# Channel mixers of a two-layer encoder trunk: two of the four weight-block sums formed on GpSimd in place of VectorE

## Chip, cores and metric

The kernel runs on one core of one Trainium2 chip. The metric is the device time of one execution in microseconds (us), the median of the runs shown. TensorE is called PE, its weight loads PEld, VectorE DVE, ScalarE ACT, GpSimd POOL and SyncE SP.

## What is computed

A trunk of two layers over 512 tokens of width 1024 in float32. Each layer has a token mixer (layer 0: a matrix memory and a memory attention; layer 1: a band attention and a memory attention) and then a channel mixer. The change lies in the channel mixers, which compute, with `D_FF` = 2816:

```
def conv_ffn(h, w_up, conv_w, conv_b, w_down):
    u, g = jnp.split(h @ w_up, 2, axis=-1)
    g = causal_dwconv(g, conv_w, conv_b)
    return (jax.nn.silu(g) * u) @ w_down
...
        x = x + conv_ffn(rmsnorm(x, norm_ffn_g[l]), ffn_w_up[l], ffn_conv_w[l], ffn_conv_b[l], ffn_w_down[l])
```

## The kernel before

**Numbers.** Every float32 operand of a matmul is split in two: a high part, rounded by ACT (a CAST, line 140), and a low part, source less high part, by DVE (line 141). Each product is then three matmuls (`mm3`, lines 194 to 196). High and low parts of weights live in tiles `wh`/`wl` or `fh`/`fl`, activations in `u`.

**The channel mixer.** The 2816 hidden columns are 22 tiles of 128 (`j` = 0 to 21). Tiles 0 to 4 are computed plainly (`plain`). Tiles 5 to 21 (`later`, one `step` each, 17 in each layer) take one level of a seven-product block scheme: the weights of the tile's up columns and gate columns are cut in halves of the inner dimension, a11 and a12 (up), a21 and a22 (gate), the activations were cut and combined once by `forms`, and seven half-size products replace eight. For that, four sums of weight blocks are formed for each tile, each 128 partitions by 512 elements, all in line 888:

- s1 = a21 + a22 (`sums`; the gate's halves)
- s2 = s1 - a11 (`sums`)
- s3 = a11 - a21 (`sum_third`; up less gate)
- s4 = a12 - s2 (`sum_fourth`)

The raw gate blocks lie in one big `pt` tile (two slots, in turn), the raw up blocks in `wr`, and the four sums in a second `pt` tile that all steps share: s1 and s3 in its first half (`s13`), s2 and s4 in its second (`s24`). So in rows of the profile `pt<-pt` is s1, `pt<-pt,wr` s2, and `pt<-wr,pt` s3 or s4.

**The order of a step.** The orders on PE, ACT and DVE are written out by hand (`tc.manual_schedule`, lines 817 to 822); POOL's and SP's orders are the scheduler's. In step j PE runs the products of tile j (call `w`), while DVE and ACT form the blocks of tile j+1 (`nxt`) and finish the outputs of tile j-1 (`tail`). PE's order: a11 into bank r1, a12 into r2, s2 into r1, s1 into r3 (`psc`), s3 into r1, down products of an earlier group (`ptr`, one of them in steps 5 to 8, two in steps 9 to 20, as the table `UNITS` gives them by tile), a22 into r1, s4 into r3. The bank r1 is used four times a step; before each new use ACT has copied it out (lines 842 and 834).

The chain that the prediction follows lies in the first half of a step and belongs to the tail: DVE adds r3 to a result (line 938) and splits s4 (line 141), then does the two taps of the convolution (line 685, two instructions); ACT then applies the SiLU (line 950) and, behind it in its queue, copies the s2 product out of r1 (line 834), upon which PE may write the s3 product into r1. Later in the step DVE forms s1 and s2 (line 888), gates (line 953), forms s3 (line 888), and splits; near its end ACT and DVE split the whole tile s13 (`split_sums`: `wh<-pt`, `wl<-pt`), then DVE forms s4, and both split the gate's half and, ahead of step 7 and of each step from 9 on, a tile of down weights (`split_down`, `wl<-wr`).

**POOL's queue.** In the mixers POOL held only DMA issues: the accumulating stores of down products (line 778, behind an ACT copy, line 777), and in steps 5 to 16 of layer 0 a pair of copies for the bias rows of layer 1 (lines 1271 and 1273, `more_rows`); the second of a pair waits until the first has landed.

Of the kernel before, what the change touches and what calls it, by code (L numbers as in the profile page):

```python
# [13 lines left out]
ALU = mybir.AluOpType  # L14
# [40 lines left out]
def trunk(  # L55
# [19 lines left out]
    V, A, G = nc.vector, nc.scalar, nc.gpsimd  # L75
# [18 lines left out]
    def ps(tag):  # L94
        count[0] += 1
        return psum.tile([P, S], F32, tag=tag, name=f"p{tag}{count[0]}", bufs=pbufs[tag])
# [6 lines left out]
    def small(n=4, dtype=F32):  # L103
# [15 lines left out]
        out=maskf, in_=maskf, pattern=[[1, P]], base=0, channel_multiplier=-1,  # L119
# [746 lines left out]
    class Forms:  # L866
# [17 lines left out]
            split(hi, lo, src)  # L884
            return hi, lo

        def sub(self, o, x, y, op=ALU.subtract):
            V.tensor_tensor(out=o, in0=x, in1=y, op=op)  # L888

        def sums(self):  # L890
            a21, a22 = self.halves(self.gate)
            s1, s2 = self.halves(self.s13)[0], self.halves(self.s24)[0]
            self.sub(s1, a21, a22, ALU.add)
            self.sub(s2, s1, self.halves(self.up)[0])

        def split_second(self):
            self.s2 = self.form(self.halves(self.s24)[0])

        def sum_third(self):
            self.sub(self.halves(self.s13)[1], self.halves(self.up)[0], self.halves(self.gate)[0])  # L900

        def split_up(self):
            self.a11, self.a12 = zip(*(self.halves(t) for t in parts(self.up, block=0)))
# [379 lines left out]
    for j in range(KT):  # L1283
        wh, wl = weights(rows(ffn_w_down[0], j * P, P, FT - LAST, FT), LAST, P)
        o = ps("mm")
# [255 lines left out]
```

## Time and profile before

| what | value |
|---|---|
| time, three runs | median 1179.55 us (1179.12 to 1180.36) |
| the profiled execution's own time | 1178.89 us |
| its span (first to last instruction) | 1177.2 us |
| PE / DVE / ACT / POOL busy in the span | 99% / 80% / 62% / 11% |
| steps of layer 0, steps of layer 1 | about 340 to 575 us, about 895 to 1128 us |
| a step with two down products, a step with one | 15.0 us, 12.3 us |

The profile is of one execution, so sums go against 1178.89 us. A row of the timeline gives the start and the duration in us, engine, line and operation, the tile written and the tiles read, and in brackets the idle time ahead of it with what ended it. Neighbouring instructions of DVE and ACT overlap by almost 0.1 us in these rows, so that 0.69 us of one is 0.61 us from start to start. Ends of matmuls are modelled: starts say more.

### The profile page before, as it was taken

The numbers are of one execution on the slowest core, as the hardware profiler recorded it, in microseconds if no ns is written. First come the engines' busy times: TensorE is split into PE (matmuls) and PEld (weight loads), VectorE is DVE, ScalarE is ACT, GpSimd is POOL, SyncE is SP. The second block draws the span as 40 slices with busy tenths as digits, with TensorE's granted clock in tenths as the row PEclk, the third lists the DMA queues.
The fourth block names the chain that finished last, engine by engine and source line by source line (L and its number), as shares of the span: only waits on it lengthen the run. The fifth ranks groups of instructions, "written<-read, shape, count | busy, mean of one in ns | idle before, by whom it ended". The sixth has DMA issues, their size and how long they took to land.

```text
span 1177.2 us, 18659 instructions
## 1 busy us (share of the span) xinstructions
PE 1167.7 (99%) x7007; PEld 1033.4 (88%) x7007; DVE 941.1 (80%) x1685; ACT 730.3 (62%) x1295; POOL 129.6 (11%) x222
## 2 busy tenths in 40 slices
PE   9999999999999999999999999999999999999997
PEld 9988888888889999999888888888889999999986
DVE  6877688887979887777698888897897887777755
ACT  6548677654656656665666667776565665666545
POOL 1111101000021111111020000101001011110100
PEclk9999999999999999999999999999999999999999
DMA  8645325243267766665564312335426456566551
GB/s 301 206 108 136 94 55 152 76 140 120 90 157 153 190 165 162 163 144 128 149 200 126 90 54 85 105 100 179 142 90 153 108 140 140 143 144 144 126 161 72
DMA packets 200445, 158.64 MB, mean 135 GB/s; under 512 B 8377, under 2 KB 180383, under 8 KB 200355
## 3 DMA queue, kind: packets, MB, share of 16 engines
q1 hardware_dynamic: 184194, 119.87, 34.5%
q0 software_dynamic: 15584, 36.67, 15.8%
q8 instruction: 55, 0.90, 0.3%
q10 hardware_dynamic: 576, 0.92, 0.2%
q14 instruction: 36, 0.29, 0.1%
HBM read 128.89 MB, written 32.46 MB: 137 GB/s over the span
## 4 chain that ended last, share of the span: by engine, by line
PE 95%; DVE 3%; ACT 1%; issue 0%; POOL 0%; POOLq 0%; DVEq 0%; ACTq 0%
PE pmm L194 18%; PE pmm L195 18%; PE pmm L196 18%; PE ptr L195 6%; PE ptr L194 6%; PE ptr L196 6%; PE psc L196 5%; PE psc L195 5%; PE psc L194 5%; PE psc L544 2%; PE ptr L1365 1%; PE ptr L1386 1%; PE ptr L1387 1%; PE ptr L627 1%; PE ptr L613 0%; DVE pt L141 0%
## 5 line engine op out<-in xcount | busy, mean ns | idle before, releaser
L194 PE MATMUL pmm<-u,wh 128*128 128x512 f32 (+1 forms) x968 | 333.0, 344 | 0.2 <-ACT u L140 0.2
L196 PE MATMUL pmm<-u,wl 128*128 128x512 f32 (+1 forms) x968 | 330.8, 342 | 0.0
L195 PE MATMUL pmm<-u,wh 128*128 128x512 f32 (+1 forms) x968 | 330.5, 342 | 0.0
L141 DVE TENSOR_TENSOR wl<-wr,wh 128x1024 fp32r<-128x1024 f32 (+3 forms) x172 | 199.8, 1163 | 82.0 <-ACT wh L140 81.5
L140 ACT CAST wh<-wr 128x1024 fp32r<-128x1024 f32 (+3 forms) x172 | 171.9, 1001 | 93.1 <-PE pmm L195 39.6
L196 PEld LDWEIGHTS pmm<-u,wl 128*128 128x128 f32 x968 | 181.9, 188 | 20.8
L194 PEld LDWEIGHTS pmm<-u,wh 128*128 128x128 f32 x968 | 181.8, 188 | 18.7 <-ACT u L140 1.1
L195 PEld LDWEIGHTS pmm<-u,wh 128*128 128x128 f32 x968 | 182.0, 188 | 18.4 <-DVE u L141 0.5
L194 PE MATMUL ptr<-u,wh 128*128 128x512 f32 x272 | 106.4, 391 | 0.0
L195 PE MATMUL ptr<-u,wh 128*128 128x512 f32 x272 | 106.2, 390 | 0.0
L196 PE MATMUL ptr<-u,wl 128*128 128x512 f32 x272 | 105.8, 389 | 0.0
L778 POOL DMA_DIRECT2D xspill<-t x64 | 55.5, 867 | 432.1 <-ACT t L777 419.6
L834 ACT COPY t<-pmm 128x256 f32<-128x256 f32 x102 | 38.2, 374 | 76.7 <-PE pmm L196 76.5
L141 DVE TENSOR_TENSOR u<-t,u 128x512 fp32r<-128x512 f32 (+1 forms) x94 | 54.2, 600 | 35.4 <-ACT u L140 35.4
L194 PE MATMUL pmm<-u,fh 128*128 128x256 f32 x272 | 75.4, 277 | 0.0
L195 PE MATMUL pmm<-u,fh 128*128 128x256 f32 x272 | 75.2, 277 | 0.0
L196 PE MATMUL pmm<-u,fl 128*128 128x256 f32 x272 | 75.1, 276 | 0.0
L196 PE MATMUL psc<-u,wl 128*128 128x256 f32 (+1 forms) x232 | 75.1, 324 | 0.0
L195 PE MATMUL psc<-u,wh 128*128 128x256 f32 (+1 forms) x232 | 75.1, 324 | 0.0
L194 PE MATMUL psc<-u,wh 128*128 128x256 f32 (+1 forms) x232 | 74.9, 324 | 0.0
L141 DVE TENSOR_TENSOR fl<-pt,fh 128x512 fp32r<-128x512 f32 x102 | 70.4, 690 | 5.1 <-ACT fh L140 1.4
L140 ACT CAST fh<-pt 128x512 fp32r<-128x512 f32 x102 | 62.8, 616 | 9.2 <-DVE pt L888 6.0
(334 smaller groups left out, 2509.1 us busy)
## 6 DMA issues: line engine op xcount, KB each, us to landing
wr<-in_ffn_w_up_dram SPq DMA_DIRECT2D x54, 512.0 KB, 6.0
wr<-in_ffn_w_down_dram SPq DMA_DIRECT2D x38, 512.0 KB, 5.5
pt<-in_ffn_w_up_dram SPq DMA_DIRECT2D x34, 512.0 KB, 7.7
xspill<-t POOLq DMA_DIRECT2D x64, 256.0 KB, 4.3
wr<-in_a_w_in_dram SPq DMA_DIRECT2D x20, 512.0 KB, 3.8
wr<-in_w_kv_dram SPq DMA_DIRECT2D x12, 512.0 KB, 4.1
xspill<-fh POOLq DMA_DIRECT2D x16, 256.0 KB, 2.6
xspill<-fl POOLq DMA_DIRECT2D x16, 256.0 KB, 3.1
```

Source lines behind the costliest of these rows:

```text
L140: high = A.copy(hi, src) if on_act else V.tensor_copy(hi, src)
L141: low = V.tensor_tensor(out=lo, in0=src, in1=f(hi), op=ALU.subtract)
L194: nc.tensor.matmul(o, lh, rh, start=first, stop=False, skip_group_check=more)
L195: nc.tensor.matmul(o, lh, rl, start=False, stop=False, skip_group_check=more)
L196: nc.tensor.matmul(o, ll, rh, start=False, stop=last, skip_group_check=more)
L544: nc.tensor.matmul(o, a, b, start=first and i == 0, stop=i == 1)
L627: nc.tensor.matmul(o2, vs[a][:, 2 * hp + h, :], p[h][:, a, :], start=i == 0, stop=i == 3)
L778: G.dma_start(xspill[j], t, accum_op=ALU.add)
L834: A.copy(o, r[:, :H])
L1365: nc.tensor.transpose(tp[:, b * P : (b + 1) * P], es[T, h][:, b * P : (b + 1) * P], ident)
L1386: nc.tensor.matmul(o2[:, s * P :], w, hi_at(pts[h], s, s, TT - s), start=s == 0, stop=False)
L1387: nc.tensor.matmul(o2[:, s * P :], w, lo_at(pts[h], s, s, TT - s), start=False, stop=s == TT - 1)
```

## The change

`sub`, the helper of line 888, takes an engine. s1 and s3 go to POOL; s2 and s4 stay on DVE. Operands, tiles and values are the same.

```
-        def sub(self, o, x, y, op=ALU.subtract):
-            V.tensor_tensor(out=o, in0=x, in1=y, op=op)
+        def sub(self, o, x, y, op=ALU.subtract, on=V):
+            on.tensor_tensor(out=o, in0=x, in1=y, op=op)
...
-            self.sub(s1, a21, a22, ALU.add)
+            self.sub(s1, a21, a22, ALU.add, G)
             self.sub(s2, s1, self.halves(self.up)[0])
...
-            self.sub(self.halves(self.s13)[1], self.halves(self.up)[0], self.halves(self.gate)[0])
+            self.sub(self.halves(self.s13)[1], self.halves(self.up)[0], self.halves(self.gate)[0], on=G)
```

34 sums s1 and 34 sums s3 leave DVE's queue and enter POOL's. PE's order is the same, ACT's the same but for one cast in layer 1 that moves ahead of a copy. Three places show the rest.

**Step 7 of layer 0, DVE** (from the second tap to the split of the up weights; `t_3869` is the tail's tile, `pt_3237` the sums, `pt_3236` the gate's blocks, `wr_3866` the up blocks):

```order
 L685 SCALAR_TENSOR_TENSOR t_3869<-t_3723,cols_799,t_3869 128x510
 L845 TENSOR_TENSOR t_3878<-t_3878,pmm_3876 128x256
-L888 TENSOR_TENSOR pt_3237<-pt_3236 128x512
 L888 TENSOR_TENSOR pt_3237<-pt_3237,wr_3866 128x512
 L953 TENSOR_TENSOR t_3869<-t_3721,t_3869 128x512
 L141 TENSOR_TENSOR fl_3939<-pt_3237,fh_3938 128x512
-L888 TENSOR_TENSOR pt_3237<-wr_3866,pt_3236 128x512
 L141 TENSOR_TENSOR u_3957<-t_3869,u_3956 128x512
 L141 TENSOR_TENSOR wl_3961<-wr_3866,wh_3960 128x1024
```

Two instructions have gone, both behind the taps of this step; nothing else moved.

**The same two sums on POOL** (tile 8's), behind the accumulating store of step 6's down product and the first copy of a bias row:

```order
 L778 DMA xspill<-t_3830 128x512
 L1271 DMA rep_3862<-in_b_rel_row_dram 128x640
+L888 TENSOR_TENSOR pt_3237<-pt_3236 128x512
+L888 TENSOR_TENSOR pt_3237<-wr_3866,pt_3236 128x512
 L1273 DMA rep_3862<-maskf 64x64
 L778 DMA xspill<-t_3987 128x512
```

Both sums stand directly behind the store that came at the end of step 6, so they may run while DVE is at the beginning of step 7. In layer 1 the order is the same without lines 1271 and 1273.

**A step with two down products, on POOL** (the sums of tile 13, formed around the start of step 12; `t_4660` and `t_4667` are the two stores of step 11):

```order
 L1273 DMA rep_4524<-maskf 64x64
 L778 DMA xspill<-t_4660 128x512
+L888 TENSOR_TENSOR pt_3237<-pt_3236 128x512
+L888 TENSOR_TENSOR pt_3237<-wr_4703,pt_3236 128x512
 L778 DMA xspill<-t_4667 128x512
```

Here the sums stand between the two stores.

**The first steps of layer 0, on POOL:**

```order
+L888 TENSOR_TENSOR pt_3237<-wr_3531,pt_3236 128x512
+L1271 DMA rep_3561<-in_b_rel_row_dram 128x640
+L1273 DMA rep_3561<-maskf 64x64
 L778 DMA xspill<-t_3475 128x512
 L778 DMA xspill<-t_3491 128x512
+L888 TENSOR_TENSOR pt_3237<-pt_3236 128x512
+L888 TENSOR_TENSOR pt_3237<-wr_3565,pt_3236 128x512
 L778 DMA xspill<-t_3511 128x512
 L778 DMA xspill<-t_3527 128x512
-L1271 DMA rep_3561<-in_b_rel_row_dram 128x640
-L1273 DMA rep_3561<-maskf 64x64
```

The first pair of bias copies has moved ahead of four stores.

## The prediction, as put on record

> **What bounds the kernel now.** I read the busy times first, then what PE waits for, then the starts of PE's matmuls.
>
> ```profile
> span 1177.2 us, 18659 instructions
> PE 1167.7 (99%) x7007; PEld 1033.4 (88%) x7007; DVE 941.1 (80%) x1685; ACT 730.3 (62%) x1295; POOL 129.6 (11%) x222
> 250.00:575.00 325.00, 324.84 (x2125) 294.91 (x2124) 268.60 (x399) 196.03 (x323) 46.37 (x64) 1.00 0.59 147
> 805.00:1125.00 320.00, 320.00 (x2090) 291.18 (x2090) 265.82 (x395) 194.38 (x320) 31.62 (x40) 1.00 0.56 136
> PE pmm L453 <- DVE mcf L127: 1.1, 1, 1.1
> PE pmm L196 <- DVE u L141: 0.4, 2, 0.2
> ```
>
> The columns of the two windows are length, then busy time (and instructions) of PE, PEld, DVE, ACT and POOL, then clock, DMA share and GB/s. They hold the mixers' steps, and PE is busy in them throughout, at a granted clock of 1.00. The last two rows are the longest waits of PE by what it waited for, 1.1 us at the start and 0.4 us. So PE is the bound; DVE, at 83% (268.6 of 325), has room on average.
>
> A busy PE can still hide small waits, as its ends are modelled. The starts tell:
>
> ```profile
> 370.44 0.28 PE L196 MATMUL psc<-u,wl 128*128 128x256 f32 x1
> 370.56 0.28 PE L194 MATMUL pmm<-u,wh 128*128 128x256 f32 x1
> ```
>
> A matmul shown as 0.28 us is followed after 0.12 by the next, here and in other steps I looked at. What PE could gain in the steps is therefore about nothing. The change can only cost, where it makes PE wait, or be hidden.
>
> **What is removed.** DVE loses 34 sums s1 and 34 of the sums in the second row:
>
> ```profile
> L888 DVE TENSOR_TENSOR pt<-pt x34: 682/684/693, 240.0 to 1111.5; 128x512 f32<-128x512 f32 x34
> L888 DVE TENSOR_TENSOR pt<-wr,pt x68: 683/686/698, 334.2 to 1119.7; 128x512 f32<-128x512 f32 x68
> ```
>
> 34 x 0.684 + 34 x 0.686 = 46.6 us of DVE. They stand behind the taps of their step, and before the next taps DVE waits for ACT anyway (rows below), so they buy PE nothing: 0 us.
>
> **What is added.** No row shows POOL adding two tensors. Nearest are a write of 512 elements and a select of 128:
>
> ```profile
> L524 POOL MEMSET u<- 64x512 f32 x24 | 12.7, 531 | 137.9 <-PE psc L544 69.9 <-PE pmm L195 40.3 <-ACT t L1354 23.0
> 190.00 0.30 POOL L1172 TENSOR_SCALAR_AFFINE_SELECT t<-t 128x128 f32<-128x128 f32 x1
> ```
>
> A sum passes 512 elements three times, two in and one out. As cheap as the memset, it takes 0.53 us; with three passes in a row, 1.6 us. I take two passes, 1.1 us (the memset is the nearest row, and a write can run beside the reads), and keep both ends. [...]
>
> At 1.1 us POOL has time. Its wait as such costs nothing if the sum is started early:
>
> ```profile
> 430.29 0.92 POOL L778 DMA_DIRECT2D xspill<-t  x1 [2.07 <-ACT t L777]
> 438.69 0.69 DVE L888 TENSOR_TENSOR pt<-pt,wr 128x512 f32<-128x512 f32 x1
> ```
>
> In step 12, s1 and s3 stand behind this store, from 431.2, and DVE needs s1 at about 438, for s2, 7 us later; s3 is needed later still. Behind the two sums wait only stores and bias copies. The first pair of copies moves ahead of two stores and makes them wait up to
>
> ```profile
> POOL rep L1273 <- DMA rep<-in_b_rel_row_dram: 84.7, 12, 8.2
> ```
>
> 8.2 us once; their buffers come back eight tiles later in the ring `t`, over a step away. I count 0; without that cover ACT's next tile would wait out the rest, at most 8 us once.
>
> **Where the two engines collide.** The same trace shows POOL and DVE getting in each other's way:
>
> ```profile
> 188.54 0.78 DVE L141 TENSOR_TENSOR u<-t,u 128x512 fp32r<-128x512 f32 x1
> 188.75 0.72 POOL L1172 TENSOR_SCALAR_AFFINE_SELECT t<-t 128x128 f32<-128x128 f32 x1
> 233.56 0.33 POOL L1172 TENSOR_SCALAR_AFFINE_SELECT t<-t 128x128 f32<-128x128 f32 x1 [1.45 <-ACT t L1170]
> 233.66 0.65 DVE L141 TENSOR_TENSOR pt<-t,pt 128x384 fp32r<-128x384 f32 x1
> L141 DVE TENSOR_TENSOR wl<-wr,wh 128x384 fp32r<-128x384 f32 x4 | 2.2, 548 | 0.0
> ```
>
> A select that takes 0.30 us alone takes 0.72 beside a DVE instruction with two inputs in SBUF, and ends 0.15 us after that one's end (189.32). The other way round, a DVE split of 384 elements behind a running select takes 0.65 in place of 0.55. I read this as taking turns: the later of the two waits for the earlier. Nearly all DVE work of a step has two such inputs. [...]
>
> So each step pays two turns of G (one sum's time) on DVE, around its beginning. PE feels it through one chain: DVE taps, ACT SiLU, ACT copy out of bank r1, PE's s3 product into r1. Its slack decides. In step 12:
>
> ```profile
> 431.13 0.69 DVE L888 TENSOR_TENSOR pt<-wr,pt 128x512 f32<-128x512 f32 x1
> 431.74 0.68 DVE L141 TENSOR_TENSOR fl<-pt,fh 128x512 fp32r<-128x512 f32 x1
> 433.68 1.23 DVE L141 TENSOR_TENSOR wl<-wr,wh 128x1024 fp32r<-128x1024 f32 x1 [1.26 <-ACT wh L140]
> 437.55 0.63 ACT L950 ACTIVATE t<-t 128x512 f32<-128x512 f32 x1 [0.97 <-DVE t L685]
> 438.92 0.37 ACT L834 COPY t<-pmm 128x256 f32<-128x256 f32 x1 [0.74 <-PE pmm L196]
> 440.08 0.28 PE L194 MATMUL pmm<-u,wh 128*128 128x256 f32 x1
> ```
>
> The SiLU ends at 438.18, the copy could start at 438.92 (0.74), and it ends at 439.29, 0.79 before PE's start: the slack is 1.53 us. The sums start when the first row ends (431.82); with a split (0.61) between them the wide split follows at 431.82 + 2G + 0.61, against 433.68 before: late by 2G - 1.25, since its wait for ACT takes up the rest. At G = 1.1 that is 0.95, under 1.53: PE waits 0. The 11 steps 10 to 20 of each layer are of this kind.
>
> Step 7 has no such gap and less slack:
>
> ```profile
> 364.54 0.89 POOL L1271 DMA_DIRECT2D rep<-in_b_rel_row_dram  x1
> 364.93 0.68 DVE L141 TENSOR_TENSOR fl<-pt,fh 128x512 fp32r<-128x512 f32 x1
> 365.53 1.22 DVE L141 TENSOR_TENSOR wl<-wr,wh 128x1024 fp32r<-128x1024 f32 x1
> 366.67 0.41 DVE L938 TENSOR_TENSOR t<-t,psc 128x256 f32<-128x256 f32 x1
> 367.00 0.69 DVE L141 TENSOR_TENSOR fl<-pt,fh 128x512 fp32r<-128x512 f32 x1
> 367.60 1.53 DVE L685 SCALAR_TENSOR_TENSOR t<-t,cols,t 128x511 f32<-128x511 f32 x2
> 369.23 0.63 ACT L950 ACTIVATE t<-t 128x512 f32<-128x512 f32 x1 [2.17 <-DVE t L685]
> 369.76 0.36 ACT L834 COPY t<-pmm 128x256 f32<-128x256 f32 x1
> ```
>
> The copy runs right behind the SiLU and ends at 370.12, 0.44 before PE's 370.56 (quoted above); the two ACT rows overlap by 0.1, so I take 0.35 as slack. s1 comes to POOL's head at 365.43 and gets its turn at 365.62; then the wide split (1.22), s3 beside line 938 (one input in PSUM), the second split (0.61), the taps: 365.62 + 2G + 1.83 against 367.60, late by 2G - 0.15; were the wide split first and s1 behind it, it would be the same. PE waits 2G - 0.5 = **1.7 us** at G = 1.1. Steps 7 and 9 of each layer are so: 4 x 1.7 = 6.8 us.
>
> Step 8 lies between:
>
> ```profile
> 377.20 0.69 DVE L141 TENSOR_TENSOR fl<-pt,fh 128x512 fp32r<-128x512 f32 x1
> 378.74 1.53 DVE L685 SCALAR_TENSOR_TENSOR t<-t,cols,t 128x511 f32<-128x511 f32 x2
> 380.37 0.63 ACT L950 ACTIVATE t<-t 128x512 f32<-128x512 f32 x1 [1.04 <-DVE t L685]
> 381.67 0.38 ACT L834 COPY t<-pmm 128x256 f32<-128x256 f32 x1 [0.67 <-PE pmm L196]
> 382.83 0.28 PE L194 MATMUL pmm<-u,wh 128*128 128x256 f32 x1
> ```
>
> Slack 0.67 + 0.78 = 1.45; the taps follow at 377.89 + 2G + 0.61, late by 2G - 0.24 = 1.96: PE waits 0.5, twice 1.0 us. Step 6 has a little more slack and an idle gap of DVE; I count it as 0.
>
> Sum: 6.8 + 1.0 = **7.8 us**. 1178.89 + 7.8 = 1186.7; the median of the three runs stands 0.66 above the profiled one, so 1187.3.
>
> **Rivals.**
>
> *No collision that matters (no change).* DVE's instructions follow each other closely, and if POOL gets in only beside those with an input in PSUM, or the two share the port finely, the delay halves: 2G becomes G, step 7 pays 0.6, the others nothing, 4 x 0.6 = 2.4 us at most, 1179.6 to 1182. It is decided in step 7: a lateness under 0.35 us there costs nothing. Against it is the select that held DVE up.
>
> *The sums are longer than I think.* With 2G - 1.25 against 1.53, the 22 wide steps begin to pay from G = 1.39. At 1.6 they pay 0.42 each, 9.2 us; steps 7 and 9 pay 2.7, 10.8 us; step 8 1.5, 3.0: 23 us, 1202.5. At G = 0.53 steps 7 and 9 pay 0.56, 2.2 us: 1181.8.
>
> *Faster.* It would need PE waits that the 46.6 us of DVE time remove. In the windows PE has none; outside the steps only the first s1 of each layer leaves DVE, 0.7 us each. Were both on the path, 1178.1. A gain of 0.2% isn't in reach by this; only waits that the starts don't show would give it.
>
> **How the numbers follow.** A measurement of this kernel can tell about 0.2%, 2.4 us, from no change. The forecast (steps 6 to 9 pay, the wide ones not or hardly; 1182 to 1195): 0.48. No collision that matters: 0.26. Long sums, over 1195: 0.22. Faster: 0.04. The range goes from 1178.5, where nothing collides, to 1205, just beyond G = 1.6; I leave out the faster case and half of the long sums, 0.15. Slower by over 0.2%: 0.48 + 0.22 = 0.70; same 0.26; faster 0.04.
>
> **What would show it.** POOL rows of line 888 near 1.1 us alone, longer beside DVE; DVE splits and taps at the start of steps lengthened by about 1 us; SiLUs of steps 7 and 9 about 2 us later against PE's s1 product, with a gap of 1.7 us between PE's starts ahead of s3, and no gap in steps 10 to 20. I am wrong if DVE rows keep their 0.69 us, if POOL's take over 1.4 us, or if PE waits elsewhere: for s2, whose DVE instruction now waits for POOL, or for a buffer.

## The result, and the profile after

The changed kernel takes 1193.9 us (median of 4 runs, 1192.43 to 1195.92), the kernel before 1179.95 (4 runs, 1179.12 to 1181.59): 1.0121 times as long, 95% interval 1.0109 to 1.0134. That is slower by 14 us, inside the range and on the side that was forecast, and about twice the forecast 7.8 us.

The page of the changed kernel, and the longest waits of PE (total us, times, longest):

```profile
span 1192.6 us, 18788 instructions
PE 1172.1 (98%) x7007; PEld 1035.7 (87%) x7007; DVE 958.0 (80%) x1617; ACT 727.3 (61%) x1295; POOL 238.0 (20%) x290
...
PE pmm L194 <- ACT t L834: 10.3, 7, 2.4
PE pmm L453 <- DVE mcf L127: 1.1, 1, 1.1
PE ptr L194 <- ACT t L777: 0.5, 1, 0.5
```

PE now waits seven times for line 834, ACT's copy out of r1: that is the chain that the prediction named. DVE never waits for a sum of POOL's: its waits for POOL, 1.3 us in all, are those for line 1172, and the kernel before has them too. DVE has 68 instructions fewer and is busy for 17 us longer (958.0 against 941.1): its rows hold time in which it was shut out. The sums, by the instructions of line 888 (shortest, median, longest ns):

```profile
L888 POOL TENSOR_TENSOR pt<-pt x34: 1285/1667/1994, 239.9 to 1120.4; 128x512 f32<-128x512 f32 x34
L888 POOL TENSOR_TENSOR pt<-wr,pt x34: 1282/1742/3829, 329.4 to 1122.0; 128x512 f32<-128x512 f32 x34
```

G, a sum's time with nobody in its way, is 1.28 us, the shortest row. A longer row isn't always a wait. The pair of step 5 of layer 1 has no DVE instruction beside it:

```profile
903.16 1.60 POOL L888 TENSOR_TENSOR pt<-pt 128x512 f32<-128x512 f32 x1
904.42 1.60 POOL L888 TENSOR_TENSOR pt<-wr,pt 128x512 f32<-128x512 f32 x1
```

Its rows show 1.60 us, but the starts lie 1.26 apart: on POOL, too, starts say more than lengths. Step 7 of layer 0, the timelines of POOL, DVE, ACT and PE:

```profile
366.82 1.62 POOL L888 TENSOR_TENSOR pt<-pt 128x512 f32<-128x512 f32 x1
368.07 1.62 POOL L888 TENSOR_TENSOR pt<-wr,pt 128x512 f32<-128x512 f32 x1
```

```profile
366.61 3.64 DVE L141 TENSOR_TENSOR fl<-pt,fh 128x512 fp32r<-128x512 f32 x1
370.17 1.21 DVE L141 TENSOR_TENSOR wl<-wr,wh 128x1024 fp32r<-128x1024 f32 x1
371.31 0.41 DVE L938 TENSOR_TENSOR t<-t,psc 128x256 f32<-128x256 f32 x1
371.64 0.68 DVE L141 TENSOR_TENSOR fl<-pt,fh 128x512 fp32r<-128x512 f32 x1
372.24 1.52 DVE L685 SCALAR_TENSOR_TENSOR t<-t,cols,t 128x511 f32<-128x511 f32 x2
```

```profile
373.86 0.63 ACT L950 ACTIVATE t<-t 128x512 f32<-128x512 f32 x1 [5.12 <-DVE t L685]
374.39 0.35 ACT L834 COPY t<-pmm 128x256 f32<-128x256 f32 x1
```

```profile
372.13 0.28 PE L196 MATMUL psc<-u,wl 128*128 128x256 f32 x1
374.80 0.38 PE L194 MATMUL pmm<-u,wh 128*128 128x256 f32 x1 [2.40 <-ACT t L834]
```

The first split of DVE takes 3.64 us in place of 0.68: it ends only when both sums have ended. By the rows it had begun first (366.61 against 366.82), and the sums took no notice of it: their starts lie 1.25 apart, as in the pair without DVE. All behind the split is late, the SiLU ends at 374.49, the copy at 374.74, and PE's starts lie 2.67 us apart where 0.11 is usual, a gap of 2.56 us. (The wait's own column, 2.40, is shorter because the end of the matmul ahead is modelled.) The same step in layer 1:

```profile
929.19 1.61 POOL L888 TENSOR_TENSOR pt<-pt 128x512 f32<-128x512 f32 x1
930.76 1.75 POOL L888 TENSOR_TENSOR pt<-wr,pt 128x512 f32<-128x512 f32 x1
```

```profile
928.96 0.68 DVE L888 TENSOR_TENSOR pt<-wr,pt 128x512 f32<-128x512 f32 x1
929.56 1.79 DVE L141 TENSOR_TENSOR fl<-pt,fh 128x512 fp32r<-128x512 f32 x1
931.27 2.31 DVE L141 TENSOR_TENSOR wl<-wr,wh 128x1024 fp32r<-128x1024 f32 x1
```

Here the two engines do take turns. DVE's s4 (928.96) had begun 0.23 us ahead of s1 and keeps its 0.68, the sums start 1.57 apart, and each of them holds one DVE instruction up by 1.1 us (1.79 for 0.68, 2.31 for 1.22); the gap is 1.82 us. Step 12 of layer 0, ACT and PE:

```profile
448.49 0.63 ACT L950 ACTIVATE t<-t 128x512 f32<-128x512 f32 x1 [1.67 <-DVE t L685]
449.17 0.38 ACT L834 COPY t<-pmm 128x256 f32<-128x256 f32 x1
```

```profile
450.21 0.28 PE L196 MATMUL psc<-u,wl 128*128 128x256 f32 x1
450.33 0.28 PE L194 MATMUL pmm<-u,wh 128*128 128x256 f32 x1
```

The SiLU ends 0.05 us ahead of the copy's start, where 0.74 were left before: the taps came 0.69 late, and PE has no gap.

Where the span's extra 15.4 us (1192.6 less 1177.2) lie, by the differences of PE's starts:

| place | us |
|---|---|
| gaps ahead of s3, layer 0, steps 6 to 9 | 0.89, 2.56, 1.43, 2.54 |
| gaps ahead of s3, layer 1, steps 6 to 9 | 0, 1.82, 0.35, 1.83 |
| the first matmul behind each of the seven, 0.11 longer | 0.8 |
| a stretch of PE at half rate (granted clock 0.57) behind the last gap of layer 0 | 1.7 |
| one gap ahead of the first down product of step 5, layer 1 | 0.7 |
| loading at the start, other from run to run | 0.6 |

They add up to 15.2; steps 10 to 20 lose nothing.

### The profile page after: what moved, and what is told of

The parts are those of the page before. It is cut to its first block, busy times and chain, and to the rows that moved or that the text cites. A ratio compares the mean times of both kernels' runs of the same rounds, so it can differ in the third digit from the quotient of the medians.

```text
span 1192.6 us, 18788 instructions
## 1 busy us (share of the span) xinstructions
PE 1172.1 (98%) x7007; PEld 1035.7 (87%) x7007; DVE 958.0 (80%) x1617; ACT 727.3 (61%) x1295; POOL 238.0 (20%) x290
## 4 chain that ended last, share of the span: by engine, by line
PE 83%; DVE 10%; ACT 3%; issue 2%; DMA 2%; SPq 0%; POOL 0%; DVEq 0%; ACTq 0%; POOLq 0%
PE pmm L194 17%; PE pmm L195 16%; PE pmm L196 16%; PE ptr L195 5%; PE ptr L194 5%; PE ptr L196 5%; PE psc L196 4%; PE psc L195 4%; PE psc L194 4%; DVE fl L141 2%; PE psc L544 2%; DVE wl L141 2%; DVE t L685 1%; DMA wr<-in_ffn_w_up_dram 1%; PE ptr L1365 1%
## 5 line engine op out<-in xcount | busy, mean ns | idle before, releaser
L141 DVE TENSOR_TENSOR wl<-wr,wh 128x1024 fp32r<-128x1024 f32 (+3 forms) x172 | 220.6, 1283 | 60.4 <-ACT wh L140 58.9
L141 DVE TENSOR_TENSOR fl<-pt,fh 128x512 fp32r<-128x512 f32 x102 | 113.7, 1115 | 7.2 <-ACT fh L140 6.4
L888 POOL TENSOR_TENSOR pt<-wr,pt 128x512 f32<-128x512 f32 x34 | 60.4, 1776 | 101.7 <-DMA wr<-in_ffn_w_up_dram 101.7
```

Of the source, the lines that this page charges most:

```text
L141: low = V.tensor_tensor(out=lo, in0=src, in1=f(hi), op=ALU.subtract)
L888: on.tensor_tensor(out=o, in0=x, in1=y, op=op)
```

## The experiments

The theory: POOL's sums read SBUF and shut out DVE instructions with two inputs there; PE pays in steps 6 to 9 alone, through taps, SiLU and the copy out of r1. Rival A: PE pays for sums that POOL delivers late. Rival B: a little is paid on all 34 steps, by stores and buffers. Edits are to the changed kernel unless the text says otherwise.

**One sum alone.** First s1 on POOL, s3 on DVE:

```
-            self.sub(self.halves(self.s13)[1], self.halves(self.up)[0], self.halves(self.gate)[0], on=G)
+            self.sub(self.halves(self.s13)[1], self.halves(self.up)[0], self.halves(self.gate)[0])
```

> Only s1 on POOL, s3 back on DVE. Theory (POOL's reads shut DVE out at the start of a step; PE pays in steps 6 to 9 through taps, SiLU and bank r1): one shut-out of about 1.3 us in place of two, so steps 7 and 9 pay about 1 us each, steps 6 and 8 next to nothing: 4 us, 1182 to 1186. Rival A (DVE, and then PE, waits for sums that POOL delivers late; s2 needs s1 at once, s3 is needed much later): nearly the whole cost, over 1190. Rival B (a little on all 34 steps, from POOL's stores and buffers): half, about 1187.

Measured: 1184.5 us against 1179.28 for the kernel before, ratio 1.0043 (1.0028 to 1.0058). Gaps ahead of s3: 1.31, 0.16 and 1.31 us in steps 7 to 9 of layer 0, 0.72, 0 and 0.72 in layer 1. Step 7 of layer 0, POOL and DVE:

```profile
365.55 1.62 POOL L888 TENSOR_TENSOR pt<-pt 128x512 f32<-128x512 f32 x1
```

```profile
365.34 2.39 DVE L141 TENSOR_TENSOR fl<-pt,fh 128x512 fp32r<-128x512 f32 x1
```

One sum holds the split up by 1.7 us here, and by 1.1 in layer 1 (1.79 at 922.29): the layers differ already with a single sum.

Then the other way round:

```
-            self.sub(s1, a21, a22, ALU.add, G)
+            self.sub(s1, a21, a22, ALU.add)
```

> Only s3 on POOL, s1 back on DVE. Theory: as with s1 alone, 1182 to 1186, since either sum reads for as long at the same place. Rival A: no cost, 1179 to 1181, as nothing needs s3 soon. Rival B: half, about 1187.

Measured: 1185.71 us, ratio 1.0053 (1.0038 to 1.0068). The gaps are those of s1 alone to 0.02 us; another 0.94 us lies ahead of the first down product of layer 1, as in the changed kernel. s3 isn't needed for 10 us and costs as much as s1: rival A falls. The two costs, 5.2 and 6.4 us, add up to less than 14: each sum alone is covered by slack, or nearly, in steps 6 and 8, and the half-rate stretch comes with both alone (with s1 alone the granted clock is 1.00 from 396 to 404 us, behind the gap of step 9 too).

**Which steps.** POOL forms the sums of tiles 11 to 21 alone, at the start of steps 10 to 20:

```
+            self.mixer, self.on = mixer, G if j > 10 else V
...
+            self.sub(s1, a21, a22, ALU.add, self.on)
...
+            self.sub(self.halves(self.s13)[1], self.halves(self.up)[0], self.halves(self.gate)[0], on=self.on)
```

> Both sums on POOL for tiles 11 to 21 alone, so that POOL adds at the start of steps 10 to 20 (22 steps in all) and not of steps 6 to 9. Theory: 1179 to 1181, no waits of PE in steps 10 to 20, about 0.8 us of slack left there. Rivals A and B: 22 of 34 parts of the cost, about 1189.

Measured: 1179.92 us, ratio 1.0005 (0.9996 to 1.0015), no gaps, 0.84 us of slack left in steps 10 to 20. Then the rest, with `G if j <= 10 else V`:

> The rest: both sums on POOL for tiles 5 to 10 alone (12 of 34). Theory: the whole cost, 1190 to 1195, in the same gaps ahead of the s3 product in steps 6 to 9. Rivals A and B: 12 of 34 parts, about 1184.5.

Measured: 1194.2 us, ratio 1.0124 (1.0109 to 1.0139), with seven gaps as long as the changed kernel's, to 0.03 us. Twelve of the 34 tiles make the whole cost, and 22 cost nothing: rival B falls.

**Collisions without relief.** POOL forms s1 and s3, and DVE forms both again in its old places:

```
-            self.sub(s1, a21, a22, ALU.add, G)
+            self.sub(s1, a21, a22, ALU.add, G); self.sub(s1, a21, a22, ALU.add)
...
+            for on in (G, V): self.sub(self.halves(self.s13)[1], self.halves(self.up)[0], self.halves(self.gate)[0], on=on)
```

> POOL forms s1 and s3 as in the change, and DVE forms both again in its old places, into the same tiles: the collisions stay, and DVE is not relieved. Theory: the cost comes from the collisions alone, and the DVE time that the change frees bought nothing: 1192 to 1197, gaps ahead of the s3 product in steps 6 to 9 as in the change. Rival A (late sums: waits for POOL's results are what costs): about the same, too, so it doesn't speak on A. Rival C (the freed DVE time did shorten something, so that the change's 1194 is a loss less a gain): over 1200.

Measured: 1194.35 us, ratio 1.0122 (1.0104 to 1.014), the change's own time. The 46.6 us of DVE that the change freed bought nothing.

**Writes without reads.** POOL writes zeros in place of the sums:

```
+            G.memset(s1, 0.0)
...
+            G.memset(self.halves(self.s13)[1], 0.0)
```

> In place of each sum POOL writes zeros to the same tile at the same place in its queue: the waits for POOL and the writes stay, the two reads go (s1 and s3 are left out, they are zero). Theory: DVE is shut out by POOL's reads, so its rows keep 0.69 us and PE has no gaps in steps 6 to 9: 1179 to 1181. Rival A (waits for POOL's results) and rival D (any work of POOL, writes as well, holds DVE up): gaps in steps 7 and 9 of some 0.5 us or more, over 1182; with A as large as in the change.

Measured: 1179.37 us, ratio 0.9999 (0.999 to 1.0008). Step 7, POOL and DVE, timelines of this run:

```profile
365.48 0.87 POOL L893 MEMSET pt<- 128x512 f32 x1
365.94 0.87 POOL L900 MEMSET pt<- 128x512 f32 x1
```

```profile
365.31 0.68 DVE L141 TENSOR_TENSOR fl<-pt,fh 128x512 fp32r<-128x512 f32 x1
365.92 1.22 DVE L141 TENSOR_TENSOR wl<-wr,wh 128x1024 fp32r<-128x1024 f32 x1
```

The memsets run right beside the two splits, and the splits keep their 0.68 and 1.22 us; the memsets' rows show 0.87 us, but their starts lie 0.46 apart, as they do in step 10, where the rows show 0.52 beside such instructions too, so nothing says that the memsets were held. Waits for POOL and writes are there as in the change; what is missing is the reads, and the cost.

**One read.** POOL copies the first input:

```
+            G.tensor_copy(s1, a21)
...
+            G.tensor_copy(self.halves(self.s13)[1], self.halves(self.up)[0])
```

> In place of each sum POOL copies its first input: one read of 512 elements in place of two (a21 stands for s1 and a11 for s3, the second terms are left out). Theory: DVE is shut out still, for the length of the copy; if a copy takes 0.5 to 0.6 us, two of them make the taps of step 7 late by about 1 us, of which 0.35 is slack: 0.6 us in steps 7 and 9, none in 6 and 8, 1181 to 1184. If only instructions with two inputs on both sides collided: 1179 to 1181.

Measured: 1183.19 us, ratio 1.0032 (1.002 to 1.0045). Copies and the split in step 7:

```profile
365.43 0.95 POOL L893 COPY pt<-pt 128x512 f32<-128x512 f32 x1
365.98 0.95 POOL L900 COPY pt<-wr 128x512 f32<-128x512 f32 x1
```

```profile
365.25 2.22 DVE L141 TENSOR_TENSOR fl<-pt,fh 128x512 fp32r<-128x512 f32 x1
```

The split takes 2.22 us, 1.54 longer, and PE's gap is 1.15 us in steps 7 and 9 of layer 0 and 0.45 in layer 1, where 0.6 was expected in both. One input on POOL's side is enough, and the cost is less where POOL reads for less time (0.61 us is the shortest copy).

**The two layers.** The twelve pairs of bias copies issued ahead of layer 0's mixer:

```
-        tc.keep_in_program_order(G.dma_start(corner, maskf[HD:, :HD]))
+        corners.append(corner)
...
+    [more_rows() for _ in range(BH)]; [tc.keep_in_program_order(G.dma_start(c, maskf[HD:, :HD])) for c in corners]; hid = channel_mixer(0, act, norm, col["gffn"][:, 0:8], lambda: None)
```

> The change, with all twelve pairs of bias copies issued ahead of layer 0's mixer and not between its sums. Layer 0's steps lost 7.4 us in gaps ahead of the s3 product and layer 1's 4.0. Theory: POOL reaches the sums 0.9 us later in layer 0, behind a copy's issue, where DVE has less idle time left; without it layer 0 loses as layer 1 does, 1.8 in steps 7 and 9, 0.3 in step 8, 0 in step 6: 4 us, so 3 to 5 us less than the change, 1189 to 1191. Rival (the layers differ for another cause): 1193 to 1195.

Measured: 1192.17 us, ratio 1.0106 (1.009 to 1.0121). The gaps of layer 0 are now 0, 1.81, 0.35 and 1.79, those of layer 1 as before: the copies that stood around the sums are what made layer 0's longer. The time misses the expectation by 1 us. PE has two new gaps, 1.7 and 0.8 us, near 314 and 321 us, without which it would not. No other run has them, and PE's waits for line 141 below are new:

```profile
PE pmm L194 <- ACT t L834: 7.0, 6, 1.7
PE psc L196 <- DVE wl L141: 1.6, 1, 1.6
...
PE pmm L196 <- DVE wl L141: 0.7, 1, 0.7
```

**The chain.** The SiLU issued behind ACT's copy of the s2 product:

```
-            A.activation(self.acc, self.acc, AF.Silu)
...
+        silu = lambda self: A.activation(self.acc, self.acc, AF.Silu)
...
-            sum_products(new.up[:, H:], r1, w.s2, 2)
+            sum_products(new.up[:, H:], r1, w.s2, 2); then(tail, "silu")
```

> The change, with ACT's SiLU issued behind its copy of the s2 product out of r1 in place of ahead of it. POOL's sums and their collisions with DVE stay. Theory (the lateness of DVE's taps reaches PE only through that copy, which queues behind the SiLU): the gaps ahead of the s3 product vanish, up to 0.3 us each may come back ahead of the a22 product, whose copy queues behind a cast that waits for s2; with the 0.9 us at the first ptr product of layer 1: 1179.5 to 1182. Rival (another chain, by banks or sums, holds PE too): gaps of 1.5 us and more stay, over 1187.

Measured: 1183.1 us, ratio 1.0032 (1.002 to 1.0044). Step 7 of layer 0, DVE and ACT, and PE's waits:

```profile
367.67 3.63 DVE L141 TENSOR_TENSOR fl<-pt,fh 128x512 fp32r<-128x512 f32 x1
```

```profile
372.13 0.37 ACT L834 COPY t<-pmm 128x256 f32<-128x256 f32 x1 [2.35 <-PE pmm L196]
374.91 0.63 ACT L931 ACTIVATE t<-t 128x512 f32<-128x512 f32 x1 [2.40 <-DVE t L685]
```

```profile
PE psc L194 <- DVE t L854: 0.9, 1, 0.9
PE ptr L194 <- ACT t L777: 0.3, 1, 0.3
```

DVE is shut out for as long as in the change (3.63), the copy no longer waits for the taps, and every gap ahead of s3 is gone. What comes next in line is another place than the one expected: the s4 product waits for line 854, DVE's read of r3, in step 7 of layer 0 (1.03 us) and a little in two more steps (0.18, 0.27). Those and 0.48 us ahead of the first down product make 2 us, and the time misses the expected range by 1.1 us. The profiled execution is the longest of the seven (1184.78 us); in it PE falls 2.8 us behind in the first 11 us, ahead of any mixer, by a wait of 2.1 us for a load (`u<-in_mem_dram`) and a lower clock (0.997 over the whole execution, where the median run has 0.999). How much of that lies in the median, 3.6 us over the kernel before, isn't known. The control, the same move in the kernel before:

> The kernel before, with the same move of the SiLU. PE has no waits in the steps to lose: 1178.5 to 1180.5 by the theory and by any rival; it is the control for the run with the change.

Measured: 1179.1 us, ratio 0.9999 (0.9989 to 1.0008). No version that was run beats the kernel before.

## Why the prediction was right, and where its sizes were off

- *PE is the bound, and freed DVE time buys nothing*: right, shown by the sums formed twice (1194.35).
- *POOL's reads shut DVE out*: right, shown by memset (1179.37 us against 1179.23, no cost) against copy (4.0 us) and sum (14 us). That line 938, with an input in PSUM, runs beside s3 unhindered, as the sum for step 7 has it, no row of the prediction shows; in the changed kernel it keeps its 0.41 us beside s3 (918.53).
- *Steps 7 and 9 pay, step 8 a little, steps 10 to 20 nothing*: right, shown by the two runs by tiles. The wide steps' taps came 0.69 us late, 0.95 were forecast.
- *G = 1.1 us*: too small as a sum's time, which is 1.28. The write that runs beside the reads fits the copy, one read and one write in 0.61 us where the memset's starts lie 0.46 apart. What a turn costs DVE is 1.1 us all the same (step 7 of layer 1), so the figure was right by luck where it counted. With it 2G - 0.5 gives 1.7 us for steps 7 and 9, and layer 1 has 1.82 and 1.83; its three gaps make 4.0 us, and the forecast has 3.9 for a layer. With 1.28 the formula gives 2.06. The slack of 0.35 was right to 0.05 us (taps 2.22 late, 1.87 due).
- *Taking turns*, the term that was mis-sized: in layer 0 DVE gave way from the start. By the prediction's reading of the selects, that the later waits for the earlier, s1 would have waited for the split that had begun, and DVE would have had a turn between the sums; instead the split ended behind both, and the taps came 2.95 us late, where that reading gives 2.05 with 1.1 us a turn. The same split gave way to s1 alone (2.39 us), so it doesn't take two sums in a row. So steps 7 and 9 lost 2.56 and 2.54 us there, step 8 1.43 in place of 0.5, and step 6, counted as 0, 0.89. The prediction saw that the copy's issue delays s1 in layer 0 (its 365.43), but took both layers to pay alike; with the copies moved they do.
- *The first pair of bias copies* moved ahead of four stores, not two as the prediction has it, and cost nothing, as counted: PE has no gap from the start of the steps to step 6.
- *ACT's order* was told as unchanged but for one cast ahead of a copy in layer 1, and got no price. The gap ahead of the first down product there, 0.7 us, is a wait for that copy (line 777). The cast's new place alone doesn't make it: the runs with a memset or a copy in place of s3 have the cast there as well and no gap, and the run with the sums formed twice has the old order and 0.22 us. Its cause is open.
- *The half-rate stretch*, 1.7 us, was in no term.

Gaps with their longer matmuls 12.2, clock 1.7, first down product 0.7: 14.6 us in the profiled execution, against 7.8. Of the 6.8 us between them 3.5 are layer 0's gaps (7.4 against 3.9) and 3.2 what no term had: the longer matmuls, the half rate and the down product. Of the rivals, late sums and wide steps that pay are excluded by the runs; "no collision that matters" and "faster" by the result.

## What to carry to other kernels

Where the bound engine is full and waits for nothing, as here, moving work off another engine can at best break even, so look for the place where the helper's work meets the chain with the least slack, and not at the average load. In these runs work on POOL that reads SBUF was paid for by DVE instructions with two inputs there: a split of 0.68 us took 3.64 beside two sums and 2.22 beside copies (line 938, with one of its inputs in PSUM, keeps its 0.41 us beside s3 at 918.53). Put such work where DVE waits anyway (here steps 10 to 20, ratio 1.0005) or let POOL only write (0.9999). Slack per step, read as the time between the end of one link and the start of the next, gave the gaps to 0.1 us from the lateness of the taps; the lateness itself was the hard part, and in layer 0 it was forecast wrong.

## What was not expected of the hardware

A DVE instruction that had begun 0.21 us ahead of a POOL instruction can be held until POOL is through, be it one sum (2.39 us for a split of 0.68) or two in a row (3.64); elsewhere one that had begun 0.23 us ahead keeps its 0.68, and DVE gets in between the two sums (1.79, then 2.31). The start of a row thus doesn't tell which engine gives way. Why it is one in layer 0 and the other in layer 1 is open, beyond that the bias copies around the sums decide it.

Behind the last gap of layer 0, PE ran at half rate. The windows of the changed kernel (length, busy us of PE, PEld, DVE, ACT and POOL, then clock, DMA share, GB/s), and its matmuls:

```profile
400.00:404.00 4.00, 1.63 (x14) 1.43 (x14) 3.96 (x8) 1.34 (x3) 0.56 (x1) 1.00 0.93 273
404.00:408.00 4.00, 4.00 (x17) 3.52 (x17) 1.77 (x4) 2.31 (x5) 0.00 (x0) 0.57 0.37 101
```

```profile
404.54 0.41 PE L195 MATMUL pmm<-u,wh 128*128 128x256 f32 x1
404.75 0.41 PE L196 MATMUL pmm<-u,wl 128*128 128x256 f32 x1
```

The granted clock is 0.57 in the second window, and matmuls start 0.21 us apart in place of 0.11, for some 3.3 us. It is there, behind the same gap of step 9, in the three profiles with the long gaps of layer 0 (the change, tiles to 10, the sums formed twice: 0.57, 0.57 and 0.58 in a window of 4 us), and it isn't behind the equally long gap of step 7, where matmuls start 0.11 apart again, nor where the gaps are 1.8 us or less (1.00 with the bias copies ahead). Why it follows the gap of step 9 in all three and not that of step 7 is open; no run here tests it. Gaps on the bound engine can thus cost more than their length, here 1.7 us more than 2.54.
